# Two padding tiles grow from 96 to 480 bytes in a transformer-block kernel on one Trainium2 core

## The chip, the core and the metric

The kernel runs on one NeuronCore of a Trainium2 chip. The core has a matrix engine (TensorE, in the profile PE for its matmuls and PEld for its weight loads), a vector engine (DVE), a scalar engine (ACT), a GpSimd engine (POOL) and a sync engine (SP), which here issues the DMAs. The on-chip memory SBUF has 128 partitions; an address below is a byte address within a partition, the same in all of them. The metric is the device time of one execution in microseconds (us). Before the change it was 1093.33 us, the median of three runs (1092.91 to 1094.55).

## The reference

One block of a hybrid transformer for a sequence of 1024 tokens of width 1024, all in float32: a normalisation, a projection, stick-breaking attention with 8 heads of 64 beside a gated linear recurrence, an output projection, and an MLP with a squared ReLU and a hidden width of 4096.

```
h = rms_norm(x, norm1_g)
q, k, v, xl, gl = split(h @ w_in)               # 1024 -> 3*512 + 2*512
attn = stick_breaking_attention(rms(q), rms(k), v)
lru  = rg_lru(conv(xl), ...) * gelu(gl)
x = x + concat(attn, lru) @ w_out               # 1024 -> 1024
h = rms_norm(x, norm2_g)
x = x + square(relu(h @ w_up)) @ w_down         # 1024 -> 4096 -> 1024
```

## The kernel before

**The products.** A float32 product is made of three matmuls in the format fp32r. Each operand X is split into a high part (a copy rounded to fp32r, on ACT) and a low part (X minus the high part, on DVE or POOL), and low times high, high times low and high times high are summed in PSUM. Nearly all of them are 128x128 weights against 128x512 moving elements. In this kernel a matmul is a pair of instructions: a weight load takes the *stationary* operand (128 partitions x 128 elements, 512 bytes a partition) into the array, then the matmul streams the *moving* operand (512 elements, 2048 bytes a partition). While one matmul streams, the weights of the next are loaded.

**The stages.** The front part (`record_front`, lines 408 to 939) makes the projections, attention, the recurrence and the output projection. There, moving and stationary operands of the large products are tiles `hTh`, `hTl` (the transposed input), `w` (the split `w_in`) and `u` (slots of 2 KB). The MLP (`record_mlp`, lines 942 to 1179) works through a scheme of Strassen type: two halves of the hidden width, and in each an up stage (PSUM tiles `p1` to `p5`) and a down stage (`pa`, `pb`, `pc`). Its 2,688 matmuls are all issued by `mms` (line 996): for each product the stationary operand is a slice of a tile `st` (weights of `w_up`, or hidden units in the down stage) and the moving operand a tile `mv` (the split activations, or weights of `w_down`). Each of these tiles holds the high and the low part, 2048 bytes each.

**The order.** `Plan.schedule` (line 233) lays all operations out with a list scheduler and its own costs before anything is built; the order on every engine, and the slot that a tile gets, come out of that plan and are pinned. A tile waits until its slot is free.

**Where the tiles lie.** Pools take SBUF from two ends: the left side grows upwards from low addresses, the right side downwards from the top. The right side begins with a pool `align` with one tile that nobody uses (line 1230), then `x1`, `hTh`, `hTl` and so on. The left side holds some constants (`const`, `small`), then the pool `fc` (line 1229) with small constants, among them a tile `falign` that nobody uses (line 1241), then `identb`, `maskb`, `zb` and the tiles of attention (`A`, `wt`, `qk`, `v`, `G`). After the front part the left pools close, and `h2`, `mv`, `st` and `ra` take their place, from where `fc` began. The MLP has 12 slots for `mv`, 8 on the left and 4 more in a pool `mv_` on the right, and 6 for `st`, 2 on the left and 4 in `st_` on the right (`COUNT`, `MORE`, lines 44 and 51). The moving operand of a transpose is the constant `ident`, on the left ahead of `fc`.

Of the kernel before, what the change touches and what calls it, by code (L numbers as in the profile page):

```python
# [10 lines left out]
F32 = mybir.dt.float32  # L11
# [9 lines left out]
P = 128  # L21
# [1163 lines left out]
def kernel(ctx, tc, x, xt, vecs, w_in, w_rg, w_ig, w_out, w_up, w_down, out):  # L1185
# [4 lines left out]
    def pool(stack, name, bufs=1, space=None, side=None):  # L1190
        kw = {} if space is None else {"space": space}
        if side is not None:
            kw["side"] = side
        if space is not DRAM:
            kw["reuse_waits"] = "tile"
        return stack.enter_context(tc.tile_pool(name=name, bufs=bufs, **kw))
# [30 lines left out]
    psums, left, right, late = ExitStack(), ExitStack(), ExitStack(), ExitStack()  # L1227
    spools = {"s2": pool(ctx, "f_s2")}
    fc = pool(left, "fc")
    pool(ctx, "align", side="right").tile([P, 24], F32, name="align")  # L1230
    E.x1 = pool(ctx, "x1", side="right").tile([P, NT, D], F32, name="x1")
    lgs = E.x1[:].rearrange("p a b -> p (a b)")
    for t in ("w", "f"):
# [4 lines left out]
    E.bd = hp.tile([P, NCT, P], F32, name="bd")  # L1238
    E.rsb = hp.tile([P, S], F32, name="rsb")
    for nm, shape in (("K1", [1056]), ("ones2", [32]), ("rstd1", [NT]), ("var1", [NT]), ("epsv", [NT]), ("gcol", [1]), ("t_a", [4]), ("t_b", [4]), ("t_c", [4]),  # L1240
                      ("sp_", [4]), ("nsp", [4]), ("falign", [24])):
        setattr(E, nm, fc.tile([P] + shape, F32, name=nm))
    E.identb = fc.tile([P, P], BF16, name="identb")
    E.maskb = fc.tile([P, P], BF16, name="maskb")
# [101 lines left out]
```

## Time and profile before

| what | value |
|---|---|
| median of three runs | 1093.33 us (1092.91 to 1094.55) |
| the profiled execution, its own time | 1093.57 us |
| its span, first to last instruction | 1091.8 us |
| DVE busy | 812.3 us (74%) |
| ACT busy | 574.9 us (53%) |
| POOL busy | 461.6 us (42%) |
| DMA | 120.82 MB, 111 GB/s over the span |

The profile is of one execution. A row of grouped instructions gives the source line (here always the helper's line 1205), the engine, the operation, the tiles that are written and read, the shape, the count, the busy time and the mean duration. A matmul's duration in the trace is from its start to a modelled end; successive matmuls overlap, so the time that a stream of them takes is read from the spacing of their starts, not from the duration.

### The profile page before, as it was taken

To read this page: it belongs to the slowest core of one execution; us is meant where nothing else is said; L and a number is where in the kernel's file an instruction comes from. 1 tells how busy PE (TensorE), PEld (TensorE's weight loads), DVE (VectorE), ACT (ScalarE), POOL (GpSimd) and SP (SyncE) were. 2 spreads that over 40 slices of the span, in tenths; PEclk is the share of its full clock that TensorE was granted. 3 is DMA by queue.
4 is the path that set the end of the run, shared out by engine and by line. 5 is a ranking of instruction groups with operands and counts; after the bars stand their busy time and mean duration, and the time that the engine had idled before them with its cause. 6 is when DMAs were issued, how large, how long until landed. Compare 5 with 4: busy or idle time off the path is not lost.

```text
span 1091.8 us, 15111 instructions
## 1 busy us (share of the span) xinstructions
PE 1070.5 (98%) x5368; PEld 856.4 (78%) x5368; DVE 812.3 (74%) x1095; ACT 574.9 (53%) x1023; POOL 461.6 (42%) x396
## 2 busy tenths in 40 slices
PE   5999999999999999999999999999999999999998
PEld 4888777779776777788888888888888888888886
DVE  6577877977877876674758888887655669788883
ACT  7754586775586543355237753444442368534431
POOL 2413012113114221177677435557565475742374
PEclk9999999999999999999999999999999999999999
DMA  9502111211118410143443254555343433435662
GB/s 287 163 15 58 31 53 30 68 35 60 41 37 285 149 40 2 43 150 106 118 130 95 94 164 125 174 145 172 99 126 106 135 91 113 125 111 174 199 195 85
DMA packets 80636, 120.82 MB, mean 111 GB/s; under 512 B 9137, under 2 KB 29105, under 8 KB 80561
## 3 DMA queue, kind: packets, MB, share of 16 engines
q1 hardware_dynamic: 80560, 119.86, 35.7%
q8 instruction: 42, 0.69, 0.3%
q14 instruction: 34, 0.27, 0.1%
HBM read 107.77 MB, written 12.06 MB: 110 GB/s over the span
## 4 chain that ended last, share of the span: by engine, by line
PE 92%; DVE 3%; DMA 2%; ACT 2%; issue 1%; SPq 0%; DVEq 0%; ACTq 0%
PE p L1205 28%; PE pa L1205 16%; PE pb L1205 8%; PE po L1205 8%; PE pq L1205 6%; PE pv L1205 4%; PE pc L1205 4%; PE pxl L1205 4%; PE pgl L1205 3%; PE z L1205 3%; PE pw L1205 3%; PE av L1205 3%; DMA x<-in_x_dram 1%; ACT x L1205 1%; PE pg L1205 1%
## 5 line engine op out<-in xcount | busy, mean ns | idle before, releaser
L1205 DVE TENSOR_TENSOR U<-p,U 128x512 f32<-128x512 f32 x80 | 54.8, 687 | 61.7 <-PE p L1205 61.5
L1205 PE MATMUL pq<-hTh,wq 128*128 128x512 f32 x256 | 87.7, 407 | 12.0 <-DVE wq L1205 9.9
L1205 PE MATMUL p<-m1t,st 128*128 128x512 f32 x384 | 91.6, 393 | 0.0
L1205 PE MATMUL p<-m0t,st 128*128 128x512 f32 x384 | 91.3, 393 | 0.0
L1205 PEld LDWEIGHTS p<-m1t,st 128*128 128x128 f32 x384 | 72.1, 188 | 16.8 <-POOL st L1205 0.2
L1205 PEld LDWEIGHTS p<-m0t,st 128*128 128x128 f32 x384 | 72.1, 188 | 16.6
L1205 DVE COPY wt<-pw 128x512 f32<-128x512 f32 (+1 forms) x80 | 50.3, 629 | 28.7 <-PE pw L1205 26.6
L1205 PE MATMUL p<-m1b,sb 128*128 128x512 f32 x288 | 68.8, 393 | 0.0
L1205 PEld LDWEIGHTS pq<-hTh,wq 128*128 128x128 f32 x256 | 49.1, 192 | 25.0 <-DVE wq L1205 9.9
L1205 PE MATMUL p<-m0b,sb 128*128 128x512 f32 x288 | 68.6, 394 | 0.0
L1205 ACT ACTIVATE G<-z,qv 128x512 f32<-128x512 f32 (+3 forms) x96 | 49.3, 579 | 29.9 <-PE z L1205 19.4
L1205 PEld LDWEIGHTS p<-m1b,sb 128*128 128x128 f32 x288 | 54.1, 188 | 12.6
L1205 PEld LDWEIGHTS p<-m0b,sb 128*128 128x128 f32 x288 | 54.0, 188 | 12.1
L1205 ACT ACTIVATE U<-U 128x512 f32<-128x512 f32 x97 | 57.3, 627 | 5.0 <-DVE U L1205 3.9
L1205 ACT ACTIVATE w<-z,qv 128x512 f32<-128x512 f32 (+3 forms) x96 | 48.2, 592 | 16.6 <-PE pw L1205 16.5
L1205 DVE TENSOR_TENSOR_SCAN G<-G,K 128x769 f32<-128x769 f32 (+3 forms) x32 | 48.3, 1522 | 6.0 <-ACT G L1205 6.0
L1205 PE MATMUL pq<-hTl,wq 128*128 128x512 f32 x128 | 50.7, 396 | 0.0
L1205 PE MATMUL pv<-wv,hTh 128*128 128x256 f32 x256 | 49.5, 287 | 0.0
L1205 PE MATMUL po<-woh,mxl 128*128 128x512 f32 x112 | 46.9, 419 | 1.5 <-DVE mxl L1205 1.5
L1205 PEld LDWEIGHTS pw<-ident,w 128*128 128x128 f32 x288 | 34.0, 140 | 18.0 <-DVE wt L1205 5.9
L1205 POOL MEMSET G<- 128x1 f32 x64 | 4.1, 98 | 103.5 <-DVE w L1205 59.9
L1205 PE MATMUL pw<-ident,w 128*128 128x128 f32 x288 | 45.6, 276 | 2.1 <-DVE wt L1205 2.1
(273 smaller groups left out, 2889.2 us busy)
## 6 DMA issues: line engine op xcount, KB each, us to landing
ro<-in_w_out_dram SPq DMA_DIRECT2D x20, 256.0 KB, 4.9
x<-in_xt_dram SPq DMA_DIRECT2D x16, 256.0 KB, 5.6
x<-in_x_dram SPq DMA_DIRECT2D x8, 512.0 KB, 5.0
wrl<-in_w_in_dram SPq DMA_DIRECT2D x32, 128.0 KB, 2.2
x<-in_x_dram SPq DMA_DIRECT2D x16, 256.0 KB, 5.6
b<-in_w_up_dram SPq DMA_DIRECT2D x16, 256.0 KB, 2.8
sa<-in_w_up_dram SPq DMA_DIRECT2D x16, 256.0 KB, 2.7
sb<-in_w_up_dram SPq DMA_DIRECT2D x16, 256.0 KB, 2.7
```

The source lines that it names most:

```text
L1205: self.last = tc.keep_in_program_order(getattr(self.eng, op)(*args, **kw))
```

## The change: two unused tiles become larger

The tile of the right side's first pool grows from 24 to 120 floats a partition, from 96 to 480 bytes, and so does `falign` on the left.

```
-    pool(ctx, "align", side="right").tile([P, 24], F32, name="align")
+    pool(ctx, "align", side="right").tile([P, 120], F32, name="align")
...
     for nm, shape in (("K1", [1056]), ("ones2", [32]), ("rstd1", [NT]), ("var1", [NT]), ("epsv", [NT]), ("gcol", [1]), ("t_a", [4]), ("t_b", [4]), ("t_c", [4]),
-                      ("sp_", [4]), ("nsp", [4]), ("falign", [24])):
+                      ("sp_", [4]), ("nsp", [4]), ("falign", [120])):
```

No instruction is added, removed or moved: the order on each of the five engines and the tiles' slots are the same in both programs. What differs is addresses. Everything on the right behind `align` lies 384 bytes lower, and everything on the left behind `falign` lies 384 bytes higher, as long as `fc` is open. The table gives start addresses in the two built programs, and their remainder modulo 512, which the offsets of 512 or 2048 bytes inside a tile don't change.

| tile | side | before | remainder | after | remainder |
|---|---|---|---|---|---|
| `mv`, slots 0 to 7 | left | 37888 to 66560 | 0 | the same | 0 |
| `st`, slots 0 and 1 | left | 70656, 74752 | 0 | the same | 0 |
| `mv`, slots 8 to 11 | right | 114560 to 126848 | 384 | 114176 to 126464 | 0 |
| `st`, slots 2 to 5 | right | 98176 to 110464 | 384 | 97792 to 110080 | 0 |
| `hTh`, `hTl` | right | 79744, 112512 | 384 | 79360, 112128 | 0 |
| `w`, `f`, `u` (split weights, `mx` and others) | right | e.g. 163712 | 384 | e.g. 163328 | 0 |
| `q`, `k`, `wt`, `A`, `v` | left | e.g. 29824 | 128 | e.g. 30208 | 0 |
| `ident` | left | 4224 | 128 | 4224 | 128 |

So in the MLP the remainders of a matmul's two operands (moving, stationary) are before the change (0, 0) for 564 matmuls, (384, 384) for 576, (0, 384) for 1,248 and (384, 0) for 300: equal for 1,140 and unequal for 1,548 of 2,688. After it they are (0, 0) for all. The large products of the front part have (384, 384) before and (0, 0) after, those of attention (128, 128) and (0, 0). The 288 transposes of attention's weights (`pw`), with `ident` moving and a tile `A` stationary, have (128, 128) before and (128, 0) after; the other transposes (`rb`, `sst`, `ht`) have (128, 384) and (128, 0).

## The prediction

> **What bounds the kernel now.** I read the page's head first, then the chain of waits, to see which engine sets the end.
>
> ```profile
> span 1091.8 us, 15111 instructions
> PE 1070.5 (98%) x5368; PEld 856.4 (78%) x5368; DVE 812.3 (74%) x1095; ACT 574.9 (53%) x1023; POOL 461.6 (42%) x396
> PEclk9999999999999999999999999999999999999999
> PE 92%; DVE 3%; DMA 2%; ACT 2%; issue 1%; SPq 0%; DVEq 0%; ACTq 0%
> ```
>
> TensorE is busy for 98% of the span and is 92% of the chain that ended last, at the full granted clock throughout. A change that moves no instruction can only gain or lose here by changing how long a matmul occupies the engine. So I went next to the MLP, 2,688 matmuls in one stream, and asked for the matmuls that fall in a long window of it (columns: window, its length, PE busy and count, granted clock, DMA share, GB/s).
>
> ```profile
> 470.00:1070.00 600.00, 600.00 (x2598) 1.00 0.44 133
> L1205 PE MATMUL p<-m1t,st 128*128 128x512 f32 x384 | 91.6, 393 | 0.0
> ```
>
> The second row is from the groups by line: no idle time before any of these 384 matmuls. The count of the window includes matmuls that reach into it over its left edge: one lasts 0.393 us, about 1.7 spacings. So the mean spacing is 600 / (2598 - 1.7) = **231.1 ns**. PE is not waiting; it runs at that pace. Is this the pace of the engine, or does something cost time in it? For that I read the timeline of PE in stretches in which all matmuls have the same remainders of their two addresses (the table of the change). The first three lie side by side and are the same kind of work.
>
> ```profile
> 471.50 11.54 PE L1205 MATMUL p<-m0b,sb 128*128 128x512 f32 x49
> 482.65 5.84 PE L1205 MATMUL p<-m0b,sb 128*128 128x512 f32 x25
> 488.11 11.54 PE L1205 MATMUL p<-m0b,sb 128*128 128x512 f32 x49
> 637.67 5.38 PE L1205 MATMUL pa<-mda,sda 128*128 128x512 f32 x23
> 1069.13 8.76 PE L1205 MATMUL pa<-mha,sha 128*128 128x512 f32 x37
> ```
>
> A row's length less the last matmul's 0.39 us, divided by the count less one, is the spacing. In rows one, three and five the moving tile is on the left (remainder 0) and the stationary one on the right (384): 11.15 / 48 = 232.3, again 232.3, and 8.37 / 36 = 232.5 ns. In row two both are on the left (0, 0): 5.45 / 24 = 227.1. In row four both are on the right (384, 384): 4.99 / 22 = 226.8. So the pace is **about 5 ns slower where the remainders differ**, whatever the common value is, before and after the same change of operands, in the up and in the down stage.
>
> **Is it the remainder?** In the MLP, unequal remainders always go with operands on different sides of SBUF, so side or distance could be the cause as well. The front part separates them: there all large products have (384, 384).
>
> ```profile
> 27.43 0.62 PE L1205 MATMUL pq<-hTh,wq 128*128 128x512 f32 x2
> ...
> 37.64 0.62 PE L1205 MATMUL pq<-hTh,wq 128*128 128x512 f32 x2
> ```
>
> Between these two starts lie 45 spacings: 10.21 / 45 = 226.9 ns. The moving operand walks through `hTh` and `hTl`, from address 79744 to 145280, which covers the whole gap between the left slots of the MLP (up to 78848) and the right ones (from 98176), while the weights stay above 163712. Neither a distance of up to 100 KB nor a boundary in that gap costs anything at equal remainders. So I take the remainder as the cause.
>
> **Settling.** How fast does a stream get to its pace after an interruption? A stretch of the output projection, all (384, 384), just behind a block of attention:
>
> ```profile
> 422.31 0.39 PE L1205 MATMUL po<-woh,mxh 128*128 128x512 f32 x1
> ...
> 424.37 0.39 PE L1205 MATMUL po<-woh,mxh 128*128 128x512 f32 x1
> ...
> 431.85 0.39 PE L1205 MATMUL po<-woh,mxh 128*128 128x512 f32 x1
> ```
>
> The first nine spacings take 2.06 us, 228.9 ns each; the 33 after them 7.48 us, 226.7 each. So an interruption costs about 9 x 2.2 = 20 ns beside its own length, and an undisturbed stream of equal remainders runs at 226.7. The streams of unequal ones don't settle: 48 in a row still average 232.3.
>
> This also explains the MLP's mean. With 1,548 unequal matmuls at 232.3, the 1,140 equal ones must average (2688 x 231.1 - 1548 x 232.3) / 1140 = 229.5: they stand in short stretches between unequal ones and rarely get to 226.7.
>
> **The change, part by part.** *The MLP* becomes one stream of (0, 0). I take 227.1 ns, the second row's spacing, which has one settling in 24; the bounds are 226.7 (never disturbed) and 229.5 (the equal ones keep today's mean, because something else disturbs them). The saving is 2688 x (231.1 - 227.1) = **10.8 us**, with bounds of 11.8 and 4.3. Of that, 1548 x 5.2 = 8.0 is from the unequal matmuls and 1140 x 2.4 = 2.7 from the others.
>
> *The front part's large products and attention's* go from equal to equal: 0.
>
> *The 288 transposes `pw`* go from equal to unequal, since `ident` stays at 128. The trace has both kinds, `pw` (equal) and `rb` (128, 384):
>
> ```profile
> 440.11 0.60 PE L1205 MATMUL pw<-ident,w 128*128 128x128 f32 x4
> 353.63 0.60 PE L1205 MATMUL rb<-ident,sq 128*128 128x128 f32 x4
> ```
>
> Both take 0.60 us for four: no difference, so 0. At most, if `pw` paid the 5.2 ns of the large ones, 288 x 5.2 = 1.5 us.
>
> *Other engines* read and write the moved tiles too. ACT's cast into `st`, to left and right slots alike, has nearly one duration (minimum, median, maximum, first and last start):
>
> ```profile
> L1205 ACT CAST st<-sc x16: 610/622/625, 497.6 to 866.1; 128x512 fp32r<-128x512 f32 x16
> ```
>
> I cost them at 0; they are hidden behind PE anyway.
>
> **Can the others keep up?** A faster PE asks for its operands earlier. Two views bear on it: who waits for whom (waited us, times, longest), and busy time in three stretches of 80 us (PE, PEld, DVE, ACT, POOL); the last two rows are from the timeline, at the tightest place.
>
> ```profile
> ACT st L1205 <- PE p L1205: 69.2, 30, 5.6
> DVE U L1205 <- PE p L1205: 61.5, 44, 3.6
> 620.00:700.00 80.00, 80.00 (x348) 65.05 (x348) 69.66 (x83) 38.05 (x67) 35.20 (x23) 1.00 0.47 142
> 880.00:960.00 80.00, 80.00 (x348) 65.09 (x347) 64.62 (x75) 57.00 (x100) 53.27 (x36) 1.00 0.38 112
> 960.00:1040.00 80.00, 80.00 (x348) 65.18 (x347) 69.05 (x92) 31.26 (x55) 26.26 (x18) 1.00 0.55 165
> 844.63 1.70 POOL L1205 TENSOR_TENSOR st<-sb,st 128x512 fp32r<-128x512 f32 x1 [1.57 <-ACT st L1205]
> 846.38 0.30 PEld L1205 LDWEIGHTS p<-m1t,st 128*128 128x128 f32 x2 [0.20 <-POOL st L1205]
> ```
>
> ACT and DVE wait for PE, so their work moves forward with it. DVE is 69.66 / 80 = 87% busy in the fullest stretch; at a pace 1.7% higher that is 89%. At 846 us a weight load waits 0.20 us for POOL's low part, which had waited for ACT; a few places like it may give back tenths. I take nothing off: the 227.1 already holds about 1.1 us over the settled 226.7.
>
> **Sum.** The profiled execution took 1093.57 us, 1.8 of it around the span. 1093.57 - 10.8 = 1082.8; it lay 0.24 above the median of the runs, so I predict **1082.5 us**.
>
> **The rivals.**
>
> *The supply becomes the bound.* If the down stage's fullest stretches, 620 to 700, 880 to 960 and 960 to 1040 us, kept today's pace because DVE sets it, 240 x 1.7% = 4.2 us of the gain would be lost: about 1087. For it: DVE's 87%. Against it: DVE still has waits for PE in there, and no matmul of these groups has idle time before it.
>
> *The two reads don't meet, and nothing changes.* The 5 ns would then come from something that goes with the placing, such as crossing between the sides, and the MLP stays at 231.1: 1093.3. For it: in the MLP side and remainder can't be told apart. Against it: the walk through `hTh` and `hTl`. A rule speaks for this rival: the Trainium skill, in "TensorE: Matmul & The Clock Gate", section "Step-by-step: what each phase is for", says that PE has two independent SBUF read ports and that loading the next weights takes no read bandwidth from the running matmul. By that, addresses could not matter; the 232.3 beside 227.1 in adjacent rows disagrees, and the measured rows decide.
>
> *Slower.* If crossing sides were the cost in the MLP, and the remainder mattered where `ident` is moving, the 288 transposes would pay: 288 x 5.2 = 1.5 us, and with each of their 80 blocks (the 80 copies `wt<-pw`) unsettling the stream behind it, 80 x 20 ns = 1.6: 1093.6 + 3.1 = 1096.7. It decides from 2.2 us, that is 7.6 ns a transpose. Against it: the equal 0.60 of `pw` and `rb`.
>
> ```profile
> L1205 DVE COPY wt<-pw x80: 525/667/694, 67.9 to 440.7; 128x512 f32<-128x512 f32 x48, 128x384 f32<-128x384 f32 x32
> ```
>
> **How the numbers follow.** Forecast 0.82, supply 0.10, no change 0.05, slower 0.03. The range runs from 1080.5 (11.8 saved, and about a microsecond more from fewer settlings elsewhere) to 1087, which takes in the supply rival; the bound of 4.3 saved (1089) and the two last rivals are left out, together under 2 in 10. A measurement of this kernel can tell about 0.2%, 2.2 us, from no change: faster 0.92, within it 0.05, slower 0.03.
>
> **What the next profile would show.** Right: some 2,644 matmuls in the window 470 to 1070 (600 / 0.2271 + 1.7) instead of 2598; the work of the 49 matmuls from 471.5 in about 11.3 us instead of 11.54; `pw` still 0.60 for four; the MLP about 11 us shorter and the front part as long as now. Supply: idle time before matmuls of the down stage, ended by DVE or POOL. No change: 232 ns in the same places although all remainders are 0. Wrong in size: streams of (0, 0) that are undisturbed and yet don't reach 227.

## The result: 13.2 us less, and the profile after

| | before | after |
|---|---|---|
| median of four runs each | 1093.63 us (1092.91 to 1094.55) | 1080.45 us (1079.89 to 1081.02) |
| ratio, 95% interval | | 0.9879 [0.9862, 0.9896] |
| the profiled execution, its own time | 1093.57 us | 1079.89 us |

The time lies 0.05 us below the range that was given, 1080.5 to 1087. A second set of runs of the same kernel, below, gave 1080.99 us. The page after, with the head, the clock and the chain of waits, and from the views by window and by line the rows that answer to those of before (windows: length, PE busy and count, clock, DMA share, GB/s):

```profile
span 1078.1 us, 15111 instructions
PE 1059.8 (98%) x5368; PEld 856.2 (79%) x5368; DVE 812.0 (75%) x1095; ACT 575.2 (53%) x1023; POOL 463.2 (43%) x396
PEclk9999999999999999999999999999999999999999
PE 91%; DVE 3%; DMA 2%; ACT 2%; issue 1%; SPq 0%; DVEq 0%; ACTq 0%
470.00:1070.00 600.00, 600.00 (x2648) 1.00 0.43 133
L1205 PE MATMUL p<-m1t,st 128*128 128x512 f32 x384 | 89.9, 389 | 0.0
```

All engines but PE have the busy time of before within 2 us; PE has 10.7 us less, for the same 5,368 matmuls. The window that held 2,598 matmuls holds 2,648: 600 / (2648 - 1.7) = 226.7 ns a matmul instead of 231.1. The timeline of PE shows it in the stretch where before slow and fast streams lay side by side:

```profile
468.71 30.54 PE L1205 MATMUL p<-m0b,sb 128*128 128x512 f32 x134
499.08 1.29 PE L1205 MATMUL p<-m0t,st 128*128 128x512 f32 x5
```

Now it is one stream: (30.54 - 0.39) / 133 = 226.7 ns, the settled pace, from end to end.

Where did the 13.7 us between the two spans come from? The first weight load of the MLP divides the program (view of one tile: minimum, median, maximum duration, first and last start). The row of before:

```profile
L1205 PEld LDWEIGHTS p<-m0b,sb x288: 187/188/192, 464.0 to 574.1; 128*128 128x128 f32 x144
```

and the row of after:

```profile
L1205 PEld LDWEIGHTS p<-m0b,sb x288: 187/188/192, 461.8 to 570.0; 128*128 128x128 f32 x144
```

From there to the end of the span it took 1091.8 - 464.0 = 627.8 us before and 1078.1 - 461.8 = 616.3 after: **11.5 us less in the MLP**. The other **2.2 us** are in the front part, for which the forecast was nothing. The experiments ask for the cause of both.

### The profile page after: what moved, and what is told of

It is laid out like the page before. It is cut to its first block, busy times and chain, and to the rows that moved or that the text cites. A ratio compares the mean times of both kernels' runs of the same rounds, so it can differ in the third digit from the quotient of the medians.

```text
span 1078.1 us, 15111 instructions
## 1 busy us (share of the span) xinstructions
PE 1059.8 (98%) x5368; PEld 856.2 (79%) x5368; DVE 812.0 (75%) x1095; ACT 575.2 (53%) x1023; POOL 463.2 (43%) x396
## 4 chain that ended last, share of the span: by engine, by line
PE 91%; DVE 3%; DMA 2%; ACT 2%; issue 1%; SPq 0%; DVEq 0%; ACTq 0%
PE p L1205 28%; PE pa L1205 16%; PE pb L1205 8%; PE po L1205 8%; PE pq L1205 6%; PE pv L1205 4%; PE pc L1205 4%; PE pxl L1205 3%; PE pgl L1205 3%; PE z L1205 3%; PE av L1205 3%; PE pw L1205 3%; DVE G L1205 1%; ACT x L1205 1%; PE pg L1205 1%
```

## Experiments on padding: which side, which difference, which value

All of these kernels have the change's instructions in the same order; only the sizes of unused tiles differ. The table gives the remainders modulo 512 in the MLP as (left, right), the time with its ratio to the kernel before, which was measured again beside each group of runs, the count of matmuls in the window 470 to 1070 us, and the part from the MLP's first weight load to the end.

| run | left, right | median us | ratio, 95% interval | count | MLP us |
|---|---|---|---|---|---|
| before, first profile | 0, 384 | 1093.63 | | 2598 | 627.8 |
| the change, first profile | 0, 0 | 1080.45 | 0.9879 [0.9862, 0.9896] | 2648 | 616.3 |
| before again | 0, 384 | 1092.65 | 0.9996 [0.9986, 1.0006] | 2598 | 627.8 |
| right side alone | 0, 0 | 1081.29 | 0.9884 [0.9866, 0.9903] | 2647 | 616.2 |
| left side alone | 0, 384 | 1093.18 | 0.9995 [0.9984, 1.0006] | 2598 | 627.8 |
| difference 256 | 0, 256 | 1080.92 | 0.9882 [0.9864, 0.9900] | 2647 | 616.3 |
| difference 128 | 0, 128 | 1093.07 | 1.0005 [0.9995, 1.0014] | 2598 | 627.8 |
| difference 64 | 0, 64 | 1093.67 | 1.0006 [0.9996, 1.0015] | 2595 | 628.5 |
| difference 32 | 0, 32 | 1094.43 | 1.0017 [1.0007, 1.0026] | 2595 | 628.6 |
| equal at 384 | 384, 384 | 1081.06 | 0.9894 [0.9878, 0.9911] | 2647 | 616.3 |
| the change again | 0, 0 | 1080.99 | 0.9893 [0.9878, 0.9909] | 2647 | 616.3 |
| ident at 0 as well | 0, 0 | 1082.08 | 0.9897 [0.9878, 0.9915] | 2647 | 616.3 |

**Before, again.** No edit.

> The kernel before once more, unchanged, to see how far the front part moves by itself. Theory D (the 2.1 us that the front part gained beside the forecast is the luck of three waits for loads: 0.8 us at the first matmul, 1.4 us at 27 us, 0.8 us at 340 us): the start of the first matmul and the waits at 27 and 340 us differ from the first profile of the same kernel by a microsecond or so in sum, and the MLP by under 0.3 us. Theory E (that gain comes from the new addresses): the front part ends at 464.0 us as in the first profile, within 0.3 us. Time: the ratio to before is 1.000 by both.

The MLP took 627.8 us to the tenth; the front part ended 1.1 us earlier than in the first profile. Rows of the same wait in three executions, first of before, which waits for DVE's low part of `q`, at 27 us:

```profile
26.86 0.50 PE L1205 MATMUL pq<-hTh,wq 128*128 128x512 f32 x1 [1.58 <-DVE q L1205]
```

of the change:

```profile
25.36 0.50 PE L1205 MATMUL pq<-hTh,wq 128*128 128x512 f32 x1 [0.19 <-DVE q L1205]
```

and of before again:

```profile
26.12 0.50 PE L1205 MATMUL pq<-hTh,wq 128*128 128x512 f32 x1 [0.54 <-DVE q L1205]
```

The same program waits 1.58 us there in one execution and 0.54 in another, and this matmul starts 0.74 us earlier in the second; in the change it started 1.50 us earlier. So about half of that lead comes without any change. Theory E falls (the front part ended at 462.9 us and not at 464.0), and theory D is borne out in part: 1.1 of the 2.2 us. The change again, below, decides on the rest.

**The right side alone.**

```
-    pool(ctx, "align", side="right").tile([P, 24], F32, name="align")
+    pool(ctx, "align", side="right").tile([P, 120], F32, name="align")
```

> Only the right side's padding grows. In the MLP all pairs are (0, 0); attention stays at (128, 128), the transposes pw too. Theory A (the remainders of the two operands count): all of the MLP's gain, 11.5 us, is there: 1082 us if the front part keeps its time of before, 1080.5 if its 2.1 us come from the loads into the right side. Theory B (what counts is crossing between the sides, and the changed kernel gained through something on the left): 1093. Spacing in the MLP's window from 470 to 1070 us: 226.7 ns by A, 231 by B.

All of the MLP's gain is there, 11.6 us, and the front part ended at 463.8 us, as before. Theory A holds; the padding on the left, half of the change, is not needed for the gain.

**The left side alone.**

```
-                      ("sp_", [4]), ("nsp", [4]), ("falign", [24])):
+                      ("sp_", [4]), ("nsp", [4]), ("falign", [120])):
```

> Only the left side's padding grows. The MLP keeps its (0, 384) and (384, 0) pairs, attention goes to (0, 0), the transposes pw to the unequal (128, 0). Theory A: the MLP stays at 231 ns, the time at 1093.5, within 0.3% of before. If the transposes paid for unequal remainders, 1095 to 1096.5. If the front part's 2.1 us came from the left side, 1091.5.

No difference that can be measured. The transposes, now unequal, still take 0.60 us for four:

```profile
439.89 0.60 PE L1205 MATMUL pw<-ident,w 128*128 128x128 f32 x4
```

**A difference of 256.** The change with 56 floats in `align` instead of 120.

> As the changed kernel, but the right side's padding is such that its remainder is 256: 1,548 MLP matmuls have operands that differ by 256 instead of 384 or 0. If the modulus is 512, the spacing in the long streams of unequal pairs is near 232 ns and the time near 1092 to 1093; if the modulus is 256 or less, 226.7 ns and 1080.5.

```profile
470.00:1070.00 600.00, 600.00 (x2647) 1.00 0.44 133
```

The 1,548 pairs are 256 bytes apart modulo 512, and run as fast as equal ones. So the modulus that counts is 256 at most; 512 is not needed. In the kernel before, 384 leaves 128 modulo 256; whether that is what made it slow is asked next.

**Differences of 128, 64 and 32.** The change with 88, 104 and 112 floats in `align`.

> The right side's remainder is 128: 1,548 MLP matmuls have operands that differ by 128. Theory A256 (equal remainders modulo 256 are what counts, after the run with a difference of 256 came out at 226.7 ns and 1080.9): as slow as a difference of 384, streams of unequal pairs at 232 ns, 1093. Theory A128 (the cost goes with something else of the old placing, and multiples of 128 are harmless): 226.7 ns and 1081.

> The right side's remainder is 64, so the operands of the 1,548 matmuls differ by 64 bytes. If any difference modulo 256 costs the same, 1093. If the cost grows with the difference (2.6 ns for half of 128), 1088. If the granule is 128 bytes and both operands only have to lie in the same part of it, 1081.

> The operands differ by 32 bytes. If any difference costs the same, 1093; if the cost grows with the difference, 1.3 ns a matmul and 1084 to 1085; if a granule of 64 or 128 bytes is what counts, 1081.

Row of the window with 128:

```profile
470.00:1070.00 600.00, 600.00 (x2598) 1.00 0.43 133
```

and with 32:

```profile
470.00:1070.00 600.00, 600.00 (x2595) 1.00 0.43 133
```

All three are as slow as before, the smaller differences a little slower still: 628.5 and 628.6 us in the MLP. In the MLP the cost doesn't grow with the difference, and it doesn't go by a granule of 64 or 128 bytes; what the sign of the difference does is shown by the bare streams below. Together with the run at 256, this leaves 256 as the modulus.

**Equal at 384.** Another 384 bytes ahead of the left pools, `align` as before.

```
+    pool(ctx, "lpad").tile([P, 96], F32, name="lpad")
     spools = {"s2": pool(ctx, "f_s2")}
...
-                      ("sp_", [4]), ("nsp", [4]), ("falign", [24])):
+                      ("sp_", [4]), ("nsp", [4]), ("falign", [120])):
```

> The common value is 384 instead of 0: the right side stays as before, and 384 bytes are put ahead of the left side's pools, so that mv, st and the tiles of attention lie at 384 too. Theory A (only the difference counts): 226.7 ns in the MLP and 1081 to 1082. Theory C (operands must begin at a multiple of 256 or 512): 231 ns or more, 1093 or slower.

616.3 us in the MLP, 2,647 matmuls in the window: at 384 as at 0 it is the equality that counts, and not the value. Theory C falls.

**The change, again.** No edit.

> The changed kernel once more, unchanged. If its first median, 1080.45, held some luck of the front part's loads, it comes out at 1081.0 within 0.5, as the other kernels with equal remainders did (1081.3, 1080.9, 1081.1); if the change gains in the front part for good, 1080.4. The MLP's stream 11.5 us shorter than before by both.

1080.99 us, some 11.7 us below the kernel before in the same round of runs (ratio 0.9893). The MLP took 616.3 us as in the first profile, but it began at 464.5 us instead of 461.8. In this execution the wait at 26 us was 1.01 us, one at 339 us (for the split of a loaded tile) 1.84 instead of 0.76, and behind it the clock fell (the timeline's row of the wait; then a window: length, PE busy and count, granted clock, DMA share, GB/s):

```profile
339.30 0.50 PE L1205 MATMUL po<-woh,mxl 128*128 128x512 f32 x1 [1.84 <-DVE mxl L1205]
...
330.00:360.00 30.00, 28.16 (x158) 0.94 0.91 320
```

against the first profile of the change:

```profile
338.08 0.50 PE L1205 MATMUL po<-woh,mxl 128*128 128x512 f32 x1 [0.76 <-DVE mxl L1205]
...
330.00:360.00 30.00, 29.24 (x174) 1.00 0.89 320
```

So the front part's gain of 2.2 us was not the change's: in the profiles of the kernels with equal remainders modulo 256 the MLP began between 461.8 and 465.1 us, in those with unequal ones between 462.9 and 464.3.

**`ident` at remainder 0 as well.** The change, with padding ahead of `ident` and of the left pools.

```
+    const.tile([P, 96], F32, name="ipad")
     ident = const.tile([P, P], F32, name="ident")
...
+    pool(ctx, "lpad").tile([P, 32], F32, name="lpad")
     spools = {"s2": pool(ctx, "f_s2")}
```

> As the changed kernel, with 384 bytes ahead of ident and 128 ahead of the left pools, so that ident also lies at remainder 0 and all 400 float32 transposes have equal pairs. If the unequal remainders of transposes cost nothing (0.60 us for four of both kinds), the time is that of the changed kernel within 0.1%. If they cost what the large ones do, 400 x 5 ns = 2 us less, and up to 1.6 us more from streams that stay settled: 1077.5 to 1079.

1082.08 us beside 1080.99 on the same chip; the intervals of the ratios lie over each other, and its profile, too, had the clock at 0.94 between 330 and 360 us. Its lowest run took 1080.14 us, still above the 1077.5 to 1079 of a gain. No gain is seen: the transposes don't pay for unequal remainders, now that both directions were tried.

## Experiments with bare streams

Two kernels hold no block at all, only streams of 96 matmuls on the same few tiles; the rows below are the timeline of PE, and a row's length less the last matmul, divided by 95, is the spacing. In the code, `st` and `mv` hold how many bytes the stationary and the moving operand lie off a multiple of 512, for even and for odd `k`.

```
for k in range(COUNT):
    s, m = st[k % 2] // size, (2048 + mv[k % 2]) // size
    nc.tensor.matmul(p[:, 0:cols], t[:, s:s + P], t[:, m:m + cols], start=k == 0, stop=k == COUNT - 1)
```

> Not the block: 21 streams of 96 matmuls each without any other work, in which only the addresses of the two operands, the format and the moving length differ; none of the reference is computed. Two theories of which pair counts. N (the weights of the next matmul are read while this one streams, so moving k against stationary k+1): the stream 'own' (own pair 128 bytes apart, next pair equal) runs at 226.7 ns, 'next' (own equal, next apart) at 232. O (a matmul's own pair): 'own' 232, 'next' 226.7. By both, 'same' and 'same_off' 226.7, 'both' 232, 'd_quarterk' (256 bytes apart) 226.7, 'd_sixtyfour' 232. Four and sixteen bytes apart: 232 if any difference counts. bf16 streams: if the cost lies in the reading of 4-byte operands, no difference between 'bsame' and 'bdiff'; else 5 ns there too. Short fp32r streams of 128 columns: no difference, as in the transposes.

```profile
29.54 21.92 PE L68 MATMUL p_same<-r 128*128 128x512 f32 x96
51.30 22.24 PE L68 MATMUL p_own<-r 128*128 128x512 f32 x96
73.38 22.10 PE L68 MATMUL p_next<-r 128*128 128x512 f32 x96
95.32 22.46 PE L68 MATMUL p_both<-r 128*128 128x512 f32 x96
117.61 21.93 PE L68 MATMUL p_same_off<-r 128*128 128x512 f32 x96
206.31 21.95 PE L68 MATMUL p_d_quarterk<-r 128*128 128x512 f32 x96
228.10 20.89 PE L68 MATMUL p_bsame<-b 128*128 128x512 bf16 x96
248.83 20.88 PE L68 MATMUL p_bdiff<-b 128*128 128x512 bf16 x96
321.92 11.76 PE L68 MATMUL p_mid_same<-r 128*128 128x256 f32 x96
333.52 11.55 PE L68 MATMUL p_mid_diff<-r 128*128 128x256 f32 x96
344.91 10.83 PE L68 MATMUL p_short_same<-r 128*128 128x128 f32 x96
355.58 10.88 PE L68 MATMUL p_short_diff<-r 128*128 128x128 f32 x96
```

By their lengths `same` and `same_off` run at 226.6 and 226.7 ns, `both` at 232.3. The effect is there with DVE, ACT, POOL and the DMAs all but idle, and it goes with how the addresses of PE's own two operands lie to each other. Neither theory of the pair holds: with the own pair apart and the next equal it is 230.0, with the own equal and the next apart 228.5. Each costs a part. In bf16 there is none: 20.89 and 20.88 us, (20.89 - 0.39) / 95 = 215.8 ns. At 256 columns of fp32r the unequal stream is even the faster by 2 ns (118.7 beside 120.8, in which stands one first spacing of 200 ns), and at 128 the two differ by half a nanosecond (111.7 and 111.1). So of what was tried, the cost belongs to fp32r matmuls with 512 columns.

> Not the block: streams of 96 fp32r matmuls of 512 columns, the moving operand 0, 32, 64, 96, 128, 160, 192, 224, 252 and 256 bytes further than the stationary one modulo 512, each followed by a stream of equal pairs; none of the reference is computed. The bare streams before showed 232.3 ns at 128 and 228.9 at 64 bytes, the MLP 231 on the mean with its mostly negative 64. Theory S (the sign counts, positive 64 being the cheaper): 64 at 228.9, 192 at 231 to 233. Theory K (the MLP's other work made 64 dearer there): 64 and 192 both at 229. By both, 0 and 256 at 226.7, and the equal streams behind settle to 226.7 within about nine matmuls.

```profile
50.93 21.92 PE L68 MATMUL p_a_zero_z<-r 128*128 128x512 f32 x96
72.69 22.57 PE L68 MATMUL p_b_thirtytwo<-r 128*128 128x512 f32 x96
95.09 21.96 PE L68 MATMUL p_b_thirtytwo_z<-r 128*128 128x512 f32 x96
116.89 22.15 PE L68 MATMUL p_c_sixtyfour<-r 128*128 128x512 f32 x96
204.90 22.55 PE L68 MATMUL p_e_half<-r 128*128 128x512 f32 x96
293.33 22.56 PE L68 MATMUL p_g_minus_sixtyfour<-r 128*128 128x512 f32 x96
315.73 21.94 PE L68 MATMUL p_g_minus_sixtyfour_z<-r 128*128 128x512 f32 x96
381.69 21.92 PE L68 MATMUL p_i_minus_four<-r 128*128 128x512 f32 x96
425.23 21.92 PE L68 MATMUL p_j_full<-r 128*128 128x512 f32 x96
```

With the moving operand further by 64 bytes a stream takes 22.15 us, by 192 (which is -64 modulo 256) 22.56: theory S holds, the sign counts. The kernel with a difference of 64 has mostly moving 0 and stationary 64, the dear direction, which fits that it gained nothing. 32, 128 and 192 all cost 0.63 to 0.65 us in 95 spacings, 6.6 to 6.8 ns each, and 96, 160 and 224 (rows not shown) 0.64 to 0.73 us; 256 costs nothing. In the first of these kernels 128 bytes cost less, 5.7 ns (232.3 beside 226.6); why the two programs differ isn't known. The equal streams behind an unequal one (`_z`) take up to 0.05 us longer than an equal one behind another: the settling.

## Why the prediction was right in kind and small in size

**What bounds it.** Right. PE sets the end before and after, and the gain in the MLP is in how long a matmul occupies it; no other engine's busy time changed by more than 2 us.

**What failed.** For the profiled execution the sum gave 1082.8 us, and it took 1079.89. Of the 2.9 us between, 0.7 are in the MLP's term and 2.2 in the front part, which was put at nothing ("go from equal to equal: 0"). The MLP's 11.5 us lie within their own bounds (4.3 and 11.8), so it was the front part that took the time out of the range.

**The remainder as the cause.** Right, and for the reason that the walk through `hTh` and `hTl` gave: right alone, equal at 384 and the bare streams exclude side, distance and value. But the modulus of 512 was taken over from the table of the change and is too large: 256 is what counts.

**The settling.** Right. Matched one by one with the addresses in the built program, the equal matmuls of the MLP before take 231.8 ns just behind an unequal one and 226.7 from the eleventh on. This is why they averaged 229.5, and why they gain too.

**The 227.1 ns.** This term was mis-sized by 0.7 us. The spacing after the change was taken from a stretch of 24 matmuls with one settling in it, as if the MLP's stream were interrupted every 24 matmuls. It isn't: the window's mean is 226.7, the bound given for a stream that is never disturbed. The term is 11.5 us (627.8 - 616.3) and not 10.8. The rows already showed no idle time before the matmuls of the MLP's large groups, so the settled value was the one to take; with it the sum gives 2688 x 4.4 = 11.8. The 0.3 us by which that is too high went to the supply, below.

**The front part at nothing.** This is the step that failed: right for what the change does there, wrong for what was measured and for the range. The sum started from one execution, whose front part took 464.0 us, and let only a microsecond be gained beside the MLP, and that by fewer settlings; in this profile 2.2 us were, by shorter waits. Executions of the same program differ there by up to 2.7 us (461.8 and 464.5 for the change), through waits for loaded data and, in two profiles, through the clock. The first set of runs of the change lay on the lucky side, 1080.45 us and the second 1080.99, and that of the kernel before on the other, 1093.63 us and later ones 1092.65 to 1093.04. So more than 1 of the 13.2 us is luck. The low end should have been 11.8 us and some 2 us of the front part's own spread below the time before.

**The transposes.** Right: 0.60 us for four, equal or not, shown in both directions, which also settles the slower rival.

**The supply.** It kept up but for 0.3 us of the 4.2 that the rival gave. The same three windows after the change (length, then busy time and count of PE, PEld, DVE, ACT, POOL):

```profile
620.00:700.00 80.00, 80.00 (x355) 66.24 (x354) 71.27 (x84) 38.00 (x68) 36.77 (x25) 1.00 0.51 160
880.00:960.00 80.00, 80.00 (x353) 65.99 (x352) 63.91 (x76) 53.86 (x95) 51.67 (x37) 1.00 0.37 112
960.00:1040.00 80.00, 80.00 (x354) 66.26 (x353) 71.23 (x90) 33.16 (x57) 29.87 (x20) 1.00 0.60 182
837.01 1.23 PEld L1205 LDWEIGHTS p<-m1t,st 128*128 128x128 f32 x6 [0.23 <-POOL st L1205]
```

DVE is 71.27 / 80 = 89% busy, as worked out, and PE is busy throughout. The tight weight load, now at 837 us, waits 0.23 us for POOL instead of 0.20. And one wait is new, at the start of a product in the second of these windows. Before:

```profile
922.54 2.74 PEld L1205 LDWEIGHTS pa<-mda,sda 128*128 128x128 f32 x12
922.77 2.93 PE L1205 MATMUL pa<-mda,sda 128*128 128x512 f32 x12
```

and after:

```profile
912.08 2.59 PEld L1205 LDWEIGHTS pa<-mda,sda 128*128 128x128 f32 x12 [0.40 <-DVE sda L1205]
912.08 3.01 PE L1205 MATMUL pa<-mda,sda 128*128 128x512 f32 x12
```

The weights come late from DVE, and these 12 matmuls take longer than before although the pace around them is higher. By the starts in the trace, one spacing of PE at 837 us is 307 ns and two at 912 are 363 and 337, together 0.33 us over three of 226.7. PE counts as busy there, since the modelled ends of its matmuls overlap, so its busy time doesn't show it. The change again has the same waits.

**No change.** This rival drew on the Trainium skill, "TensorE: Matmul & The Clock Gate", section "Step-by-step: what each phase is for": loading the next weights takes no read bandwidth from the running matmul. The bf16 streams agree (215.8 ns equal or not); the fp32r streams don't (226.7 and 232.3).

Open: that the two reads collide was not shown, only that the relation of their addresses counts; and why the own and the next pair each cost something, no run here tells.

## What to carry to other kernels

Where PE is busy all the time, its pace is worth a look of its own: divide a window by its count of matmuls, do the same for streams of one kind, and if two streams of the same shape differ, compare their operands' addresses. For streams of fp32r matmuls with 512 columns, put moving and stationary operands at equal addresses modulo 256; one unused tile at the head of a pool does it. The bf16 streams, the short fp32r streams and the transposes of this case didn't need it. And a sum that starts from one profiled execution inherits that execution's luck: a range should hold what the untouched parts vary from run to run.

## What was not expected of the hardware

- The pace of an fp32r stream with 512 columns depends on the operands' addresses modulo 256, by up to 10 ns in 226.7; that of bf16 streams (215.8 ns) doesn't.
- The dependence isn't symmetric: 64 bytes further costs 2.4 ns a matmul, 64 bytes less 6.7, while 32 bytes cost the same both ways. A few bytes are the extreme: the stream with the moving operand 4 bytes further ran at 236.7 ns, with 16 bytes at 231.6, the one with 4 bytes less (252) as fast as an equal one.

```profile
139.38 22.89 PE L68 MATMUL p_d_four<-r 128*128 128x512 f32 x96
```

- An equal stream that comes from an unequal one (32 to 224 bytes apart) needs three to ten matmuls to reach its pace, without any wait in between.
- The wait of PE near 340 us was followed by a granted clock of 0.94 over a window of 30 us where it took 1.84 us (the change again) and 1.72 us (`ident` at 0), and by the full clock where it took 0.76 us (the change), 1.54 us (before) and 1.68 us (right side alone). Within that window the clock of the change again was 0.50 from 342 to 344 us. That the wait was the cause is not shown.
